# Running sums of the layer norms in PSUM tiles of half the tokens, and a third buffer for modulation columns

## The chip, the cores and the metric

The kernel runs on one core of one Trainium2 chip, as one launch. The metric is the device time of that launch in microseconds, as the median of several runs. The engines of the core are TensorE (PE), VectorE (DVE), ScalarE (ACT), GpSimd (POOL) and SyncE (SP), which here issues the transfers. Each has its own queue and works through it in order; a semaphore tells one engine that another has finished a step. SBUF is the working memory of 128 partitions, PSUM the memory that PE writes its products to. PSUM has eight banks, and one bank holds a tile of 128 x 512 fp32 numbers.

## The reference

Two post-norm layers over 512 tokens of 1024 channels, with fp32 data. Layer 0 mixes the tokens with two recurrent heads (SSD and HGRN2), layer 1 with a convolution module; each is followed by a gated MLP with a 3 x 3 convolution over the token grid. The vectors m (scales, shifts and gates per channel, "modulation") come from a conditioning vector. What matters here is cut from it:

```python
s_c = jax.nn.silu(c)
for l in range(DEPTH):
    m = (s_c @ ada_w[l] + ada_b[l]).reshape(-1, 6, 1, D_MODEL)
    h = modulate(x, m[:, 0], m[:, 1])
    ...  # y = mixer(h) for l = 0, convolution module for l = 1
    x = layer_norm(ALPHA * x + m[:, 2] * y, post_ln_g[l, 0], post_ln_b[l, 0])
    x = layer_norm(ALPHA * x + m[:, 5] * conv_glu_ffn(modulate(x, m[:, 3], m[:, 4]), ...),
                   post_ln_g[l, 1], post_ln_b[l, 1])
return x
```

So there are four layer norms over the channels, each behind a matrix product whose result is scaled by a modulation vector and added to x. A fifth norm lies inside the convolution module and isn't touched by the change.

## The kernel before

x lies transposed in SBUF: channels on the partitions, in KT = 8 blocks of 128 channels x T = 512 tokens (`self.x[:, i, :]`). The program runs through the stages mixer, MLP of layer 0, convolution module, MLP of layer 1. Every matrix product keeps fp32 accuracy by three matmuls of rounded numbers (`mm3w`, lines 214 to 216): high weight x high input, high weight x low input, low weight x high input.

**Weights.** They stream through in tiles of 128 x 512 (four blocks of 128 x 128, in the order in which PE uses them), numbered over the whole program. `_wload` issues the load on SP (line 182, tile `wraw`), casts the high part on ACT (line 184, `whi`) and subtracts on POOL (line 188, `wlo = wraw - whi`, two inputs in SBUF). There are six buffers of each kind, so a tile's load waits until the tile six before has been worked up, and a cast until PE has used the tile six before.

**Modulation.** One column of m is 512 KB of weights, 128 x 1024 numbers. Its load is issued on SP (line 270, tile `ada`, from the pool `adap`), and DVE multiplies it by the conditioning and sums it in one instruction (line 273). During the output product of the mixer (`wout`, 16 blocks of input) twelve columns are made (`ADA_OUT`). `adap` has two buffers there (line 799).

**A norm.** For each block i of 128 channels, `fm` or `group` makes the product in a PSUM bank (tiles `ps` or `psg`; `psh` for half the tokens) of the pool `mm`, which has five banks. In the output product all five are used at once, by the blocks 0 to 4 (NW1 = 5, tiles `psg`); block 5 is the first that needs one of them again. `residual` (line 909, DVE) makes x = ps * m + x. `ln_add` collects what the norm needs: ACT squares the block (line 929, tile `sq`; for block 0 straight into the sum, line 926), and DVE adds the block to a1 (line 930) and the square to a2 (line 931). a1 and a2 are SBUF tiles of 128 x 512, so both inputs of these adds lie in SBUF. The last blocks (2 in the output and down products, 4 in the second convolution product `cw2`) are made by halves of 256 tokens: first all of them for tokens 0 to 255, then for 256 to 511. In the second half, or during the next product, hooks (`stats_later`) place the first half's statistics between PE's matmuls.

**Statistics.** `ln_sums` sums a1 and a2 over the partitions with eight small matmuls by a column of ones (line 945, tile `sm` in PSUM); DVE makes the mean and 1/sqrt(variance) from them with 15 tiny instructions (lines 948 to 951 and 256 to 261, tiles `st` and `rs`). `ln_spread` lets PE turn `st` and `rs` into a tile `pb` in PSUM that holds them for all partitions (line 961). `pb` has two slots in the pool `lnps`, of one bank each, one for each half of the tokens. `normalise` in `post` then goes through the blocks: DVE x - pb and x * pb (lines 1031, 1032), ACT the scaled and shifted high part `h1hi` (line 1034) and the whole number `h` in PSUM (line 1038; line 1036 on DVE for some), DVE the low part `h1lo = h - h1hi` (line 1039). With the first of them the next product's `group` starts (tiles `psg`).

What stands in which order on each engine is decided by the tile framework's scheduler from its own costs and the pools' buffers, apart from the hooks.

Of the kernel before, what the change touches and what calls it, by code (L numbers as in the profile page):

```python
# [147 lines left out]
class Net:  # L148
# [645 lines left out]
    def merge(self, mx, ox, y, o, so, acth):  # L794
# [4 lines left out]
        self.adap = op.enter_context(self.pool("adap", 2))  # L799
# [59 lines left out]
        ln = self.ln_start()  # L859
        for i in range(NW1):  # L860
            self.ln_add(ln, i, self.residual(bk[i], 0, 2, i))
# [7 lines left out]
    def project(self, ln, w, act, kt, layer, j, tail, then=None, first=0):  # L869

        tail, keep = tail
        for i in range(first, KT - tail):
            ps = self.fm(self.mm, w, i * P, act, kt=kt)
            self.ln_add(ln, i, self.residual(ps, layer, j, i))
            if then:
                then(i)
        last = range(KT - tail, KT)
        kept = {}
        ln.append([])
        for t0, t1 in HALVES:  # L880
            for i in last:
                ps = self.mm.tile([P, t1 - t0], F32, tag="mm", name="psh")
                blocks = kept.get(i) or [self.wblock((w, k * P, i * P)) for k in range(kt)]
                if i >= KT - keep:
                    kept[i] = blocks
                for k in range(kt):
                    self.mm3w(ps, blocks[k], [a[:, t0:t1] for a in act(k)], k == 0, k == kt - 1)
                self.ln_add(ln, i, self.residual(ps, layer, j, i, t0, t1), t0, t1)
            if t1 < T:
                self.stats_later(ln, t0, t1, 9, 12)  # L890
            last = last[::-1]
        self.flush()
# [19 lines left out]
    def ln_start(self):  # L912
        a1 = self.work.tile([P, T], F32, tag="a1", name="a1", bufs=1)
        a2 = self.work.tile([P, T], F32, tag="a2", name="a2", bufs=1)
        return [a1, a2, {}]

# [19 lines left out]
    def ln_sums(self, ln, t0, t1):  # L936
# [5 lines left out]
        sm = self.lnps.tile([P, 3 * n], F32, tag="sm", name="sm")  # L942
        for j, a in enumerate((a1, a2)):
            for c in range(n):
                nc.tensor.matmul(sm[:, j * n + c:j * n + c + 1], a[:, t0 + c * P:t0 + (c + 1) * P], self.ones[:, 0:1], start=True, stop=True)
# [107 lines left out]
    def ffn(self, layer):  # L1053
# [31 lines left out]
        ln = self.ln_start()  # L1085
# [6 lines left out]
    def conformer(self):  # L1092
# [106 lines left out]
        ln = self.ln_start()  # L1199
        for i in range(NC1):  # L1200
            self.ln_add(ln, i, self.residual(bk[i], 1, 2, i))
# [58 lines left out]
```

## Time and profile before

| | |
|---|---|
| median of 3 runs | 1749.44 us (1749.41 to 1750.38) |
| profiled execution | 1749.62 us |
| its span, first to last instruction | 1747.9 us |
| mean granted clock of PE | 0.993 |
| PE busy | 1702.3 us |
| DVE busy | 1243.4 us |
| ACT busy | 849.8 us |
| POOL busy | 523.9 us |
| line 188 on POOL | 380 tiles, 1330 ns each |
| bytes moved | 192 MB on SP's queue |

In rows of the profile a first number is the start in us from the start of the span, then the duration, the engine, the line, the operation, "out<-in" by the program's names with shapes (partitions x elements), and in brackets the idle time before it and what ended that. Rows of a line's view give the number of instructions, their shortest, median and longest duration in ns, and where the first and the last start. Rows of a stretch of time give its length and the busy time of PE, PE's weight loads, DVE, ACT and POOL (number of instructions in brackets), then the granted clock of PE, the DMA's share and GB/s.

### The profile page before, as it was taken

Reading aid. Unit: us, or ns where it says so; the run is one execution under the profiler, and the core shown is the slowest. Engines: PE = TensorE matmul, PEld = TensorE weight load, DVE = VectorE, ACT = ScalarE, POOL = GpSimd, SP = SyncE. Lnnn points to the kernel's source line nnn. Section 1 sums busy time; section 2 is a strip of 40 time slices with the busy share of each in tenths; the row PEclk is TensorE's granted clock in tenths of the full one; section 3 lists DMA queues with packets and bytes.
Section 4 is the critical chain, followed back from the end, with each engine's and each line's share of the span. In section 5 each row is a group of like instructions: output and inputs, shape, how many; then the busy total and the mean of one; then the engine's idle time right before and its main releaser. Section 6 shows DMA issues by size and latency. Waiting matters only on the chain.

```text
span 1747.9 us, 26471 instructions
## 1 busy us (share of the span) xinstructions
PE 1702.3 (97%) x9574; PEld 1461.9 (84%) x9574; DVE 1243.4 (71%) x2380; ACT 849.8 (49%) x1714; POOL 523.9 (30%) x434
## 2 busy tenths in 40 slices
PE   7999999999999999999999999999999899999997
PEld 5987768989999998798888888988899788888886
DVE  7778987979696894678777741478888876666124
ACT  3556775444444453355434322399635643333223
POOL 4400000000000001545444444533425344444453
PEclk9999999999999999999999999999999999999998
DMA  9721102444444235634334343321213233333332
GB/s 363 241 70 49 31 19 90 145 142 149 132 147 132 96 103 155 213 88 130 110 109 123 110 134 96 109 73 55 61 31 89 87 93 97 98 98 98 97 97 79
DMA packets 92194, 194.02 MB, mean 111 GB/s; under 512 B 10496, under 2 KB 13568, under 8 KB 92064
## 3 DMA queue, kind: packets, MB, share of 16 engines
q1 hardware_dynamic: 92016, 192.21, 35.5%
q8 instruction: 75, 1.23, 0.3%
q14 instruction: 55, 0.45, 0.1%
q0 software_dynamic: 48, 0.13, 0.0%
HBM read 190.21 MB, written 2.10 MB: 110 GB/s over the span
## 4 chain that ended last, share of the span: by engine, by line
PE 88%; DVE 6%; DMA 1%; ACT 1%; issue 1%; POOL 0%; ACTq 0%; POOLq 0%; DVEq 0%
PE ps L214 18%; PE ps L216 18%; PE ps L215 18%; PE lev L744 3%; PE psz L234 2%; PE psz L235 2%; PE psz L233 2%; PE seg L645 2%; PE psh L214 2%; PE psh L216 2%; PE psh L215 2%; PE psg L215 1%; PE psv L234 1%; PE psv L235 1%; PE psv L233 1%; DMA ada<-adaw 1%
## 5 line engine op out<-in xcount | busy, mean ns | idle before, releaser
L188 POOL TENSOR_TENSOR wlo<-wraw,whi 128x512 fp32r<-128x512 f32 x380 | 503.7, 1330 | 1183.0 <-ACT whi L184 1158.9
L184 ACT CAST whi<-wraw 128x512 fp32r<-128x512 f32 x488 | 300.6, 619 | 494.6 <-PE ps L215 243.3
L214 PE MATMUL ps<-h1hi,whi 128*128 128x512 f32 x768 | 299.1, 389 | 0.8 <-DVE acc L1076 0.8
L216 PE MATMUL ps<-h1hi,wlo 128*128 128x512 f32 x768 | 299.1, 389 | 0.3 <-POOL wlo L188 0.3
L215 PE MATMUL ps<-h1lo,whi 128*128 128x512 f32 x768 | 298.9, 389 | 0.0
L1076 DVE SCALAR_TENSOR_TENSOR acc<-ps,pcol,acc 128x441 f32<-128x441 f32 (+2 forms) x320 | 222.3, 695 | 57.2 <-ACT acc L1068 47.7
L216 PEld LDWEIGHTS ps<-h1hi,wlo 128*128 128x128 f32 x768 | 144.2, 188 | 31.0 <-POOL wlo L188 1.2
L214 PEld LDWEIGHTS ps<-h1hi,whi 128*128 128x128 f32 x768 | 144.2, 188 | 30.8 <-issue 1.6
L215 PEld LDWEIGHTS ps<-h1lo,whi 128*128 128x128 f32 x768 | 144.2, 188 | 29.4
L273 DVE CUSTOM_DVE_ANT_0 junk<-ada,sc,pcol 128x1024 bf16<-128x1024 f32 x80 | 107.7, 1346 | 16.8 <-DMA ada<-adaw 16.8
L909 DVE SCALAR_TENSOR_TENSOR x<-ps,mod,x 128x512 f32<-128x512 f32 x14 | 10.5, 750 | 140.2 <-PE ps L216 140.2
L188 DVE TENSOR_TENSOR wlo<-wraw,whi 128x512 fp32r<-128x512 f32 x108 | 73.9, 691 | 42.5 <-ACT whi L184 42.1
L214 PE MATMUL ps<-ghi,whi 128*128 128x512 f32 x264 | 102.7, 389 | 0.0
L215 PE MATMUL ps<-glo,whi 128*128 128x512 f32 x264 | 102.7, 389 | 0.0
L216 PE MATMUL ps<-ghi,wlo 128*128 128x512 f32 x264 | 102.7, 389 | 0.0
L1168 DVE SCALAR_TENSOR_TENSOR cr<-u,pcol,cr 128x511 f32<-128x511 f32 (+20 forms) x156 | 98.0, 703 | 1.4 <-ACT cr L1151 1.2
L214 PE MATMUL ps<-hhi,whi 128*128 128x512 f32 x240 | 97.9, 408 | 0.0
L215 PE MATMUL ps<-hlo,whi 128*128 128x512 f32 x240 | 96.7, 403 | 0.0
L216 PE MATMUL ps<-hhi,wlo 128*128 128x512 f32 x240 | 96.2, 401 | 0.0
L987 DVE TENSOR_TENSOR glo<-acc,ghi 128x512 fp32r<-128x512 f32 x44 | 55.8, 1268 | 28.2 <-ACT ghi L986 28.0
L233 PE MATMUL psz<-whi,hhi 128*128 128x256 f32 (+1 forms) x224 | 67.6, 302 | 0.0
L234 PE MATMUL psz<-wlo,hhi 128*128 128x256 f32 (+1 forms) x224 | 67.3, 301 | 0.0
(358 smaller groups left out, 4153.1 us busy)
## 6 DMA issues: line engine op xcount, KB each, us to landing
wraw<-wst SPq DMA_DIRECT2D x488, 256.0 KB, 2.6
ada<-adaw SPq DMA_DIRECT2D x104, 512.0 KB, 3.6
xk<-xT SPq DMA_DIRECT2D x8, 256.0 KB, 7.7
x<-xT SPq DMA_DIRECT2D x8, 256.0 KB, 5.1
out<-n SPq DMA_DIRECT2D x16, 128.0 KB, 1.7
xk<-ctxT SPq DMA_DIRECT2D x8, 128.0 KB, 4.0
sc<-rows SPq DMA_DIRECT2D x1, 512.0 KB, 3.6
scc<-rows SPq DMA_DIRECT2D x1, 512.0 KB, 7.5
```

Of the source, the lines that this page charges most:

```text
L184: nc.scalar.copy(hi, raw)
L188: eng.tensor_tensor(out=lo, in0=raw, in1=hi.bitcast(F32), op=ALU.subtract)
L214: mm(ps, w[0], a[0], start=start, stop=False)
L215: mm(ps, w[0], a[1], start=False, stop=False)
L216: mm(ps, w[1], a[0], start=False, stop=stop)
L233: mm(ps, a[0], w[0], start=start, stop=False)
L234: mm(ps, a[0], w[1], start=False, stop=False)
L235: mm(ps, a[1], w[0], start=False, stop=stop)
L273: nc.vector.tensor_tensor_reduce(out=junk, in0=raw, in1=self.sc if cond is None else cond, scale=1.0, scalar=self.pc("adab", n), op0=ALU.m ...
L987: return nc.vector.tensor_tensor(out=lo, in0=x, in1=hi.bitcast(F32), op=ALU.subtract)
L1076: nc.vector.scalar_tensor_tensor(out=o, in0=grid(pg)[:, r0 + dy - 1:r1 + dy - 1, c0 + dx - 1:c1 + dx - 1], scalar=wcol(dy, dx), in1=o, op0 ...
L1168: nc.vector.scalar_tensor_tensor(out=acc[:, t0:t1], in0=u[:, t0 + d:t1 + d], scalar=self.pc("cdw", tap * 8 + i), in1=acc[:, t0:t1], op0=AL ...
```

## The change

The functions `lnp_start` and `lnp_add` are new and take the place of `ln_start` and `ln_add` in the four norms above. The sums are kept in two PSUM tiles `ap`, one for each half of the tokens, with the tag `pb`: they lie in the slots in which the broadcasts of the same norm come to lie later. Each tile holds the sum of x in its first 256 columns and that of the squares in the others. A block of 512 tokens is now added by four DVE instructions of 256 columns (lines 940 and 941, two each) where there were two of 512; block 0's square is written by two ACT instructions. The last block's add of each half writes its sums to SBUF (`a1`, `a2`), where the matmuls of `ln_sums` read them. Over the program 36 adds of 512 columns and 40 of 256 become 112 of 256. The second part is one number: `adap` has three buffers in the output product. Lines behind the new functions stand 29 further down.

```diff
--- before.py
+++ after.py
@@ -796,7 +796,7 @@
         TT = nc.vector.tensor_tensor
         op = self.stack()
         mp = op.enter_context(self.pool("mop"))
-        self.adap = op.enter_context(self.pool("adap", 2))
+        self.adap = op.enter_context(self.pool("adap", 3))
         ohi = mp.tile([P, 16, T], F32R, name="ohi")
         olo = mp.tile([P, 16, T], F32R, name="olo")
         ps_ = self.stack()
@@ -856,9 +856,9 @@
         for k in range(KT):
             nc.sync.dma_start(out=self.x[:, k, :], in_=self.A["xT"][k])
             nc.scalar.mul(self.x[:, k, :], self.x[:, k, :], ALPHA)
-        ln = self.ln_start()
+        ln = self.lnp_start()
         for i in range(NW1):
-            self.ln_add(ln, i, self.residual(bk[i], 0, 2, i))
+            self.lnp_add(ln, i, self.residual(bk[i], 0, 2, i))
         self.project(ln, "wout", lambda k: (ohi[:, k, :], olo[:, k, :]), 16, 0, 2, TAIL_W, first=NW1)
         op.close()
         mx.close()
@@ -871,7 +871,7 @@
         tail, keep = tail
         for i in range(first, KT - tail):
             ps = self.fm(self.mm, w, i * P, act, kt=kt)
-            self.ln_add(ln, i, self.residual(ps, layer, j, i))
+            self.lnp_add(ln, i, self.residual(ps, layer, j, i))
             if then:
                 then(i)
         last = range(KT - tail, KT)
@@ -885,7 +885,7 @@
                     kept[i] = blocks
                 for k in range(kt):
                     self.mm3w(ps, blocks[k], [a[:, t0:t1] for a in act(k)], k == 0, k == kt - 1)
-                self.ln_add(ln, i, self.residual(ps, layer, j, i, t0, t1), t0, t1)
+                self.lnp_add(ln, i, self.residual(ps, layer, j, i, t0, t1), t0, t1, last=i == last[-1])
             if t1 < T:
                 self.stats_later(ln, t0, t1, 9, 12)
             last = last[::-1]
@@ -910,9 +910,35 @@
         return self.x[:, i, :]
 
     def ln_start(self):
+
         a1 = self.work.tile([P, T], F32, tag="a1", name="a1", bufs=1)
         a2 = self.work.tile([P, T], F32, tag="a2", name="a2", bufs=1)
         return [a1, a2, {}]
+
+    def lnp_start(self):
+
+        a = [self.lnps.tile([P, 2, T // 2], F32, tag="pb", name="ap", bufs=2) for _ in HALVES]
+        o = [self.work.tile([P, T], F32, tag=tag, name=tag, bufs=1) for tag in ("a1", "a2")]
+        return [a, [t[:].rearrange("p (j t) -> p j t", j=2) for t in o], {}]
+
+    def lnp_add(self, ln, i, r, t0=0, t1=T, last=False):
+        nc = self.nc
+        a, o, rs = ln[:3]
+        if t0 == 0:
+            rs[i] = r
+        sq = None
+        if i:
+            sq = self.work.tile([P, t1 - t0], F32, tag="t", name="sq")
+            nc.scalar.activation(out=sq, in_=r[:, t0:t1], func=AF.Square)
+        for (h0, h1), ah, oh in zip(HALVES, a, o):
+            if not t0 <= h0 < t1:
+                continue
+            if not i:
+                nc.scalar.activation(out=ah[:, 1, :], in_=r[:, h0:h1], func=AF.Square)
+                continue
+            out = oh if last else ah
+            nc.vector.tensor_tensor(out=out[:, 0, :], in0=rs[0][:, h0:h1] if i == 1 else ah[:, 0, :], in1=r[:, h0:h1], op=ALU.add)
+            nc.vector.tensor_tensor(out=out[:, 1, :], in0=ah[:, 1, :], in1=sq[:, h0 - t0:h1 - t0], op=ALU.add)
 
     def ln_add(self, ln, i, r, t0=0, t1=T, eng=None):
         nc = self.nc
@@ -940,6 +966,9 @@
         n = (t1 - t0) // P
 
         sm = self.lnps.tile([P, 3 * n], F32, tag="sm", name="sm")
+        if isinstance(a2, list):
+            both, t0 = a2[t0 > 0], 0
+            a1, a2 = both[:, 0, :], both[:, 1, :]
         for j, a in enumerate((a1, a2)):
             for c in range(n):
                 nc.tensor.matmul(sm[:, j * n + c:j * n + c + 1], a[:, t0 + c * P:t0 + (c + 1) * P], self.ones[:, 0:1], start=True, stop=True)
@@ -1082,7 +1111,7 @@
                 self.next_x(i - 1)
             if layer == DEPTH - 1 or i % 3 == 0:
                 self.ada_some(1)
-        ln = self.ln_start()
+        ln = self.lnp_start()
         self.project(ln, f"dn{layer}", lambda k: (ghi[:, k, :], glo[:, k, :]), FT, layer, 5, TAIL_D, lambda i: self.ada_some(0 if layer or i > 3 else self.ADA_DOWN))
         fx.close()
         self.hx.close()
@@ -1196,9 +1225,9 @@
             add(*HALVES[1])
             self.stats_later(ln, *HALVES[1], 8, 9, lambda p: normed(*HALVES[1], p))
         bk = self.group("cw2", [i * P for i in range(NC1)])
-        ln = self.ln_start()
+        ln = self.lnp_start()
         for i in range(NC1):
-            self.ln_add(ln, i, self.residual(bk[i], 1, 2, i))
+            self.lnp_add(ln, i, self.residual(bk[i], 1, 2, i))
         self.project(ln, "cw2", self.act, KT, 1, 2, TAIL_C, first=NC1)
         cx.close()
         self.hx.close()
```

The order of PE's matmuls is the same but for some transposes, and POOL's is the same. What moves on SP and DVE is shown at two places.

SP's queue in the output product, from weight tile 143 on (`wraw143`; `ada82` to `ada87` and `ada72` to `ada75` are the third to the twelfth of the twelve modulation columns, `x` blocks of x that are loaded there). Before:

```order
L182 DMA wraw143_7447<-wst 128x512
L270 DMA ada82_7293<-adaw 128x1024
L270 DMA ada83_7297<-adaw 128x1024
L182 DMA wraw144_7465<-wst 128x512
L182 DMA wraw145_7483<-wst 128x512
L270 DMA ada84_7301<-adaw 128x1024
L270 DMA ada85_7305<-adaw 128x1024
L182 DMA wraw146_7501<-wst 128x512
L857 DMA x_7278<-xT 128x512
L270 DMA ada86_7309<-adaw 128x1024
L270 DMA ada87_7313<-adaw 128x1024
L182 DMA wraw147_7519<-wst 128x512
```

With the change:

```order
L182 DMA wraw143_7447<-wst 128x512
L270 DMA ada83_7297<-adaw 128x1024
L270 DMA ada84_7301<-adaw 128x1024
L270 DMA ada85_7305<-adaw 128x1024
L270 DMA ada86_7309<-adaw 128x1024
L270 DMA ada87_7313<-adaw 128x1024
L270 DMA ada72_7317<-adaw 128x1024
L270 DMA ada73_7321<-adaw 128x1024
L270 DMA ada74_7325<-adaw 128x1024
L270 DMA ada75_7329<-adaw 128x1024
L182 DMA wraw144_7465<-wst 128x512
L182 DMA wraw145_7483<-wst 128x512
```

The third column's load, `ada82`, has moved up, ahead of weight tile 128. The nine others now stand in one piece ahead of weight tile 144, the first that block 5 uses; before, they alternated with the tiles 144 to 148 and with blocks of x.

DVE's queue where the first half of the second convolution product's norm is applied and the second half's residuals come in (`rs` is 1/sqrt(variance) of the first half; `a_13559` and `a_13560` are a1 and a2, `a_13588` is both). Before:

```order
L261 SCALAR_TENSOR_TENSOR rs<-vt,sm 128x2
L1031 TENSOR_TENSOR x<-x,pb 128x256
L1032 TENSOR_TENSOR x<-x,pb 128x256
L1031 TENSOR_TENSOR x<-x,pb 128x256
L909 SCALAR_TENSOR_TENSOR x<-psh,mod,x 128x256
L1032 TENSOR_TENSOR x<-x,pb 128x256
L930 TENSOR_TENSOR a_13559<-a_13559,x 128x256
L931 TENSOR_TENSOR a_13560<-a_13560,sq 128x256
L1031 TENSOR_TENSOR x<-x,pb 128x256
L1032 TENSOR_TENSOR x<-x,pb 128x256
L1031 TENSOR_TENSOR x<-x,pb 128x256
```

With the change:

```order
L261 SCALAR_TENSOR_TENSOR rs<-vt,sm 128x2
L1060 TENSOR_TENSOR x<-x,pb 128x256
L1061 TENSOR_TENSOR x<-x,pb 128x256
L909 SCALAR_TENSOR_TENSOR x<-psh,mod,x 128x256
L1060 TENSOR_TENSOR x<-x,pb 128x256
L940 TENSOR_TENSOR ap<-ap,x 128x256
L1061 TENSOR_TENSOR x<-x,pb 128x256
L941 TENSOR_TENSOR ap<-ap,sq 128x256
L1060 TENSOR_TENSOR x<-x,pb 128x256
L1061 TENSOR_TENSOR x<-x,pb 128x256
L909 SCALAR_TENSOR_TENSOR x<-psh,mod,x 128x256
```

The residual of the second to last half block stands one row earlier, and its two adds stand between instructions of `normalise` where they stood behind each other; the instructions themselves are the same in number here.

## The prediction

> **What bounds the kernel now.** I read the page first, then the list of waits on TensorE (PE), then the time line at each wait.
>
> ```profile
> span 1747.9 us, 26471 instructions
> PE 1702.3 (97%) x9574; PEld 1461.9 (84%) x9574; DVE 1243.4 (71%) x2380; ACT 849.8 (49%) x1714; POOL 523.9 (30%) x434
> ```
>
> PE is busy for 97% of the span. The change takes no matmul away, so it can only give back PE's waits, and the time in which PE ran at a low clock. The waits list (releaser; us in total, times, longest):
>
> ```profile
> PE pb L961 <- DVE rs L261: 5.0, 4, 2.3
> PE sm L945 <- DVE a L930: 4.5, 3, 1.9
> PE ps L214 <- DVE x L909: 3.9, 1, 3.9
> PE psg L214 <- ACT h1hi L1034: 3.4, 3, 1.6
> ```
>
> These 16.8 us, with the half-clock time behind them, are all that can be won. The third row is one stall after the output product; the others are in the norms.
>
> **Part 1, the third modulation buffer.** The stall, with the work before it on DVE:
>
> ```profile
> 693.42 1.27 DVE L273 CUSTOM_DVE_ANT_0 junk<-ada,sc,pcol 128x1024 bf16<-128x1024 f32 x1
> ...
> 724.79 1.28 DVE L273 CUSTOM_DVE_ANT_0 junk<-ada,sc,pcol 128x1024 bf16<-128x1024 f32 x1 [1.43 <-DMA ada<-adaw]
> ...
> 726.00 2.06 DVE L909 SCALAR_TENSOR_TENSOR x<-psg,mod,x 128x512 f32<-128x512 f32 x3
> ```
>
> ```profile
> 726.89 0.47 PE L214 MATMUL ps<-ohi,whi 128*128 128x512 f32 x1 [3.94 <-DVE x L909]
> ```
>
> All five banks of the matmul pool hold products. The next one (block 5) waits until the residual of bank 0 has read it, and that stands on DVE behind twelve reductions, which wait for their loads: 14.2 us in all.
>
> ```profile
>   DMA ada<-adaw: 14.2, 9
> ...
> DMA to landing us min/median/max: 3.4/4.3/5.5
> ```
>
> ```profile
> wraw<-wst SPq DMA_DIRECT2D x11, 256.0 KB, 4.8
> ```
>
> (The last row is of the weight tiles in 690 to 727: count, size, us to landing.) With two buffers a load starts when the reduction two before has ended, so two loads take about 4.3 + 1.3 us, 2.8 each. With three it is (4.3 + 1.3)/3 = 1.9 us. The third load is now on its way before 691, the fourth starts at 693.4, when the first reduction has ended and the second starts, and lands at 697.7. Eight more at 1.9 us and 1.3 for the last end the chain at about 714. Is there bandwidth for it?
>
> ```profile
> 690.00:727.00 37.00, 33.06 (x147) 27.06 (x146) 22.60 (x33) 11.74 (x21) 19.14 (x11) 1.00 0.83 268
> 0.00:20.00 20.00, 7.86 (x22) 5.74 (x22) 9.14 (x14) 8.71 (x12) 9.74 (x12) 1.00 0.85 318
> ```
>
> Nine loads of 0.52 MB in 20 us are 236 GB/s, below the 268 of this window and the 318 of the start, and no weight tile is interleaved with them any more. Bank 0 is complete some 2.7 us before the other four, at 720.2, its residual takes 0.75, and PE arrives at 722.96: the cover is 2 us of PE, and six more before the chain is late. What is late next is weight tile 144, the first of block 5: it now stands on SP behind all twelve loads. Its issue comes when reduction 9 has ended, about 708; the tiles landed in 4.8 us here (median), and a cast and a subtraction follow, the one on POOL of 1.3 us as below, so it is ready at 715, 8 us ahead. Tiles 145 to 148 follow at a bandwidth that brings 0.26 MB in 1 us, against 2.7 us of PE for each; the x blocks behind them are needed only after 724. The stall of 3.9 us goes. Behind it PE ran at half clock:
>
> ```profile
> 727.60:731.00 3.40, 3.40 (x9) 2.68 (x9) 3.40 (x4) 1.65 (x4) 2.44 (x2) 0.51 0.39 122
> ...
> 1140.70:1144.10 3.40, 3.40 (x18) 3.40 (x17) 2.97 (x16) 2.86 (x9) 0.00 (x0) 0.50 0.24 78
> 1365.80:1369.20 3.40, 3.40 (x19) 3.34 (x18) 3.32 (x12) 3.34 (x8) 0.00 (x0) 0.52 0.01 2
> ```
>
> (The eighth number is the granted clock.) 3.4 us at half clock cost 1.7. With no stall before it, I count that as gained: **5.6 us**; bounds 0 (rival A) and 5.7.
>
> **Part 2, the sums in PSUM.** Why do the sums delay PE? DVE's adds of two SBUF tiles are stretched:
>
> ```profile
> L930 DVE TENSOR_TENSOR a<-a,x x34: 414/693/1766, 729.6 to 1733.5; 128x256 f32<-128x256 f32 x20, 128x512 f32<-128x512 f32 x14
> L931 DVE TENSOR_TENSOR a<-a,sq x42: 407/679/1789, 729.0 to 1734.1; 128x256 f32<-128x256 f32 x24, 128x512 f32<-128x512 f32 x18
> L1039 DVE TENSOR_TENSOR h1lo<-h,h1hi x48: 408/424/426, 763.4 to 1386.6; 128x256 fp32r<-128x256 f32 x48
> L909 DVE SCALAR_TENSOR_TENSOR x<-psh,mod,x x20: 471/483/486, 745.4 to 1733.0; 128x256 f32<-128x256 f32 x20
> L1138 DVE SCALAR_TENSOR_TENSOR u<-ps,pcol,sg x7: 739/750/759, 1165.0 to 1280.6; 128x512 f32<-128x512 f32 x7
> ```
>
> The same 256 columns take 0.41 us or up to 1.5. L1039 and L909, which have one operand in PSUM (h lies there), never vary. The time line shows who stretches them:
>
> ```profile
> 1135.59 2.52 POOL L188 TENSOR_TENSOR wlo<-wraw,whi 128x512 fp32r<-128x512 f32 x2 [0.21 <-ACT whi L184]
> ...
> 1136.02 0.42 DVE L1039 TENSOR_TENSOR h1lo<-h,h1hi 128x256 fp32r<-128x256 f32 x1
> ...
> 1137.41 0.98 DVE L930 TENSOR_TENSOR a<-a,x 128x256 f32<-128x256 f32 x1
> ```
>
> While POOL subtracts (1135.59 to 1138.11, two tiles), L1039 runs at full speed, and L930, both inputs in SBUF, ends only after it. The new adds each have one input in PSUM. The price of one that also writes PSUM over 256 columns is not in the trace. Below it is bounded by L1039's 0.42, above by L1138, which reads and writes PSUM over twice the columns, 0.75. L909 is nearest in size: I take 0.46.
>
> The full-width adds, 36 of 512 columns, become 72: 36 x (0.92 - 0.68) = 8.6 us more on DVE if none had been stretched. That lies under PE, for whose products DVE waits 140 us at L909:
>
> ```profile
> L909 DVE SCALAR_TENSOR_TENSOR x<-ps,mod,x 128x512 f32<-128x512 f32 x14 | 10.5, 750 | 140.2 <-PE ps L216 140.2
> ```
>
> Only the sums that PE waits for count.
>
> *Down product of layer 0* (the sums' tile in 1124 to 1140, and PE's wait):
>
> ```profile
> L930 DVE TENSOR_TENSOR a<-a,x x2: 983/1227/1471, 1127.7 to 1137.4; 128x256 f32<-128x256 f32 x2
> L931 DVE TENSOR_TENSOR a<-a,sq x2: 407/958/1509, 1129.1 to 1138.6; 128x256 f32<-128x256 f32 x2
> ```
>
> ```profile
> 1138.54 0.58 PE L945 MATMUL sm<-ones,a 128*128 128x1 f32 x4 [1.93 <-DVE a L930]
> ```
>
> Three adds of 1.47, 1.51 and 0.98 us, 3.96, become 1.38: 2.6 us come back, and the wait of 1.93 goes. The half-clock stretch at 1140.7 follows it, with no other wait inside; I count 1.2 of its 1.7. **3.1** (0 to 3.6).
>
> *Second convolution product.*
>
> ```profile
> 1352.98 1.45 DVE L930 TENSOR_TENSOR a<-a,x 128x256 f32<-128x256 f32 x1
> ...
> 1354.42 1.46 DVE L931 TENSOR_TENSOR a<-a,sq 128x256 f32<-128x256 f32 x1
> ...
> 1358.70 1.31 DVE L930 TENSOR_TENSOR a<-a,x 128x256 f32<-128x256 f32 x1
> 1359.94 1.50 DVE L931 TENSOR_TENSOR a<-a,sq 128x256 f32<-128x256 f32 x1
> ```
>
> ```profile
> 1356.39 0.43 PE L961 MATMUL pb<-tri,rs 128*128 128x128 f32 x2 [2.01 <-DVE rs L261]
> 1361.79 0.62 PE L214 MATMUL psg<-h1hi,whi 128*128 128x256 f32 x3 [1.14 <-ACT h1hi L1034]
> 1363.76 1.02 PE L945 MATMUL sm<-ones,a 128*128 128x1 f32 x8 [1.35 <-DVE a L930]
> ```
>
> The first pair stands inside the chain that makes rs: 2.0 us shorter, which is PE's 2.01. The second pair delays the last residual and its add: of the 1.35 about 1.15 go, since the square on ACT is still behind h1hi. The 1.14 stays: ACT makes h1hi after a cast that waits for PE itself. Half of the 1.7 us of half clock at 1365.8: 0.85. **4.0** (0 to 4.9).
>
> *Output product.*
>
> ```profile
> 758.82 1.40 DVE L931 TENSOR_TENSOR a<-a,sq 128x256 f32<-128x256 f32 x1
> ...
> 765.84 1.50 DVE L931 TENSOR_TENSOR a<-a,sq 128x256 f32<-128x256 f32 x1
> ```
>
> ```profile
> 760.35 0.43 PE L961 MATMUL pb<-tri,rs 128*128 128x128 f32 x2 [0.52 <-DVE rs L261]
> ```
>
> The two stretched adds hold up rs and sums; beside the 0.52 PE waits 0.29 and 0.16 in the same time line. **1.0**; the 1.6 us for h1hi at 777 follows the broadcast directly and stays.
>
> *Last product.* L909, L930 and L931 start last at 1733.0, 1733.5 and 1734.1, one behind the other, unstretched: **0**.
>
> The broadcasts need the sums' slots free; each half's last add has read its slot before its sums start, so no wait is added.
>
> By the Trainium skill (TensorE: Matmul & The Clock Gate, What's actually happening) the clock drops after an idle window of a free-running 3.4 us. The stretches above lie on such a grid and are as long, which agrees; but the waits of 1.93 and 1.35 us fill no whole window, so by the rule's words their stretches need not go with them, and the sum would be 2.05 smaller. No row decides it.
>
> Against the change speaks VectorE: DVE Perf Modes (the TRN2 errata section) of the Trainium skill: a fixed cost falls on each instruction, so tiles of 512 are better than two of 256. Two adds of 0.41 against one of 0.68 agree. On the path the sum would lose a further 36 x 0.14 = 5 us; the 140 us of waiting for PE say that it is off it.
>
> **Sum.** 5.6 + 3.1 + 4.0 + 1.0 = 13.7 us. The profiled execution took 1749.62 us (span 1747.9), the median is 1749.44, 0.2 below: **1735.7 us**.
>
> **Rivals.**
> A. *The stall stays*: the loads get no faster (two in flight already share 268 GB/s), or tile 144 comes as late as bank 0 did. For it: 0.83 of the DMA's time is busy. Against: 318 GB/s elsewhere. Then 8.1 us: 1741.3.
> B. *PSUM adds cost 0.75.* A pair takes 1.5 instead of 0.9, and half of the norms' gain goes; the last product loses 0.65. I make it 5.6 + 2.3 + 1.4 + 0.5 - 0.65 = 9.2: 1740.3.
> C. *The norms gain nothing*, because the chain over ACT (h1hi, h, each waiting for DVE and back) takes the wait's place. For it: three waits on h1hi, 3.4 us. Against: the sums wait for adds, not for ACT. Then 5.6: 1743.8.
> D. *Slower: an add that reads and writes one PSUM bank takes 1.0 us or more.* In the second convolution product 20 adds stand before the first sums; unstretched, DVE has some 5 us to spare there, so beyond 0.46 + 5/20 = 0.7 us each the sums come late, 6 us at 1.0; the output product has 24 and loses 2.4, the end and the second halves 3. With 5.6 gained at the stall it decides from about 0.9; at 1.0 about +6: 1755. Against: L1138 takes 0.75 for twice the columns.
>
> **Chances.** Forecast 0.60, A 0.13, B 0.14, C 0.08, D 0.05. The forecast's own range is 1732 to 1739; with A and B, 1732 to 1742.5. A change within 0.2%, 3.5 us, can't be told from none: faster than 1745.9 holds for all but D and the late part of C: 0.92; same 0.04; slower 0.04.
>
> **What would show it.** The new adds at 0.42 to 0.50 us with no stretched ones; no wait of PE on L909 near 723 and full clock after it; reductions ended by about 714; the sums' waits at 1138 and 1363 and the broadcast's at 1356 gone, that for h1hi still there; the end from the last matmul unchanged. Wrong: adds above 0.7, a wait of PE on a weight's cast or subtraction near 723, or half-clock stretches that stay.

## The result

The changed kernel takes **1734.76 us** (median, 1734.36 to 1736.75), the kernel before, measured beside it, 1749.43 us (1745.98 to 1750.38): a ratio of 0.9912, with an interval of 0.99 to 0.9925. The forecast was 1735.7 us. The profiled execution took 1734.44 us with a span of 1732.7, 15.2 less than before.

The page of the kernel after, its head:

```profile
span 1732.7 us, 26538 instructions
PE 1696.8 (98%) x9574; PEld 1458.9 (84%) x9574; DVE 1220.2 (70%) x2416; ACT 849.9 (49%) x1718; POOL 520.0 (30%) x434
```

DVE has 36 instructions more and is busy 23 us less. PE is busy for 5.5 us less with the same matmuls; two stretches at half clock fewer make 3.4 us of it. The list of PE's waits (releaser; us in total, times, longest):

```profile
PE psg L214 <- ACT h1hi L1063: 4.3, 3, 1.6
PE pb L990 <- DVE rs L261: 2.1, 1, 2.1
PE pc L214 <- DVE cr L1202: 2.0, 1, 2.0
PE sm L974 <- DVE a L940: 1.1, 1, 1.1
```

The wait on L909 is gone from the list. Of the four waits for rs and the three for the sums one each is left, both in the last norm. The waits for h1hi have grown from 3.4 to 4.3.

The new adds, by line (shortest, median, longest in ns):

```profile
L940 DVE TENSOR_TENSOR ap<-ap,x x40: 417/425/433, 727.7 to 1710.7; 128x256 f32<-128x256 f32 x40
L940 DVE TENSOR_TENSOR ap<-x x8: 418/886/1522, 724.9 to 1627.1; 128x256 f32<-128x256 f32 x8
L940 DVE TENSOR_TENSOR a<-ap,x x8: 415/424/425, 745.9 to 1718.4; 128x256 f32<-128x256 f32 x8
L941 DVE TENSOR_TENSOR ap<-ap,sq x48: 415/423/433, 727.0 to 1711.6; 128x256 f32<-128x256 f32 x48
```

With one input in PSUM no add takes over 0.433 us. Only the second row's eight, block 1's x added to block 0's, still have both inputs in SBUF, and they are still stretched, to 1.52.

The output product, by stretches of time (PE, its weight loads, DVE, ACT, POOL; clock, DMA share, GB/s), and DVE's time line there:

```profile
690.00:727.00 37.00, 37.00 (x165) 30.61 (x164) 26.75 (x36) 14.33 (x27) 18.98 (x13) 1.00 0.81 270
727.00:733.00 6.00, 6.00 (x28) 4.98 (x27) 6.00 (x17) 2.54 (x5) 3.85 (x4) 1.00 0.81 268
```

```profile
699.62 2.13 DVE L273 CUSTOM_DVE_ANT_0 junk<-ada,sc,pcol 128x1024 bf16<-128x1024 f32 x1
701.84 2.32 DVE L273 CUSTOM_DVE_ANT_0 junk<-ada,sc,pcol 128x1024 bf16<-128x1024 f32 x1
...
716.18 1.28 DVE L273 CUSTOM_DVE_ANT_0 junk<-ada,sc,pcol 128x1024 bf16<-128x1024 f32 x1 [2.34 <-DMA ada<-adaw]
...
720.39 2.10 DVE L909 SCALAR_TENSOR_TENSOR x<-psg,mod,x 128x512 f32<-128x512 f32 x3 [2.92 <-PE psg L216]
```

PE is busy for all of the 37 us and at full clock behind them. The order has turned round: the residual of bank 0 now waits 2.92 us for PE's product.

PE's rows in the down product of layer 0 and in the second convolution product, where waits stood before:

```profile
1129.00 0.51 PE L974 MATMUL sm<-ones,a 128*128 128x1 f32 x4
```

```profile
1343.47 0.38 PE L990 MATMUL pb<-tri,rs 128*128 128x128 f32 x2
...
1348.58 0.62 PE L214 MATMUL psg<-h1hi,whi 128*128 128x256 f32 x3 [1.14 <-ACT h1hi L1063]
1349.04 0.95 PE L974 MATMUL sm<-ones,a 128*128 128x1 f32 x8
...
1358.40 0.38 PE L990 MATMUL pb<-tri,rs 128*128 128x128 f32 x2
1360.38 0.62 PE L214 MATMUL psg<-h1hi,whi 128*128 128x256 f32 x3 [1.60 <-ACT h1hi L1063]
```

The waits of 1.93, 2.01 and 1.35 us have gone, the 1.14 stays, and the last wait is 1.60 where it was 0.65 before:

```profile
1375.80 0.61 PE L214 MATMUL psg<-h1hi,whi 128*128 128x256 f32 x3 [0.65 <-ACT h1hi L1034]
```

Where the 15.2 us came from is read off by taking the same matmul in both traces (a stage's first `sm` or `ps`), and how much earlier it starts:

| matmul | before | after | earlier by | gained in between | predicted |
|---|---|---|---|---|---|
| first sums of the output norm | 754.25 | 748.46 | 5.79 | 5.8 | 5.6 |
| first `ps` behind that norm | 799.62 | 792.05 | 7.57 | 1.8 | 1.0 |
| first sums of down product 0 | 1120.74 | 1113.17 | 7.57 | 0 | 0 |
| first sums in the convolution module | 1310.85 | 1299.87 | 10.98 | 3.4 | 3.1 |
| first sums behind `cw2` | 1348.67 | 1337.69 | 10.98 | 0 | 0 |
| first sums of down product 1 | 1718.85 | 1703.75 | 15.10 | 4.1 | 4.0 |
| end of the span | 1747.9 | 1732.7 | 15.2 | 0.1 | 0 |

### The profile page after: what moved, and what is told of

Same layout as the page of the kernel before. It is cut to its first block, busy times and chain, and to the rows that moved or that the text cites. A ratio compares the mean times of both kernels' runs of the same rounds, so it can differ in the third digit from the quotient of the medians.

```text
span 1732.7 us, 26538 instructions
## 1 busy us (share of the span) xinstructions
PE 1696.8 (98%) x9574; PEld 1458.9 (84%) x9574; DVE 1220.2 (70%) x2416; ACT 849.9 (49%) x1718; POOL 520.0 (30%) x434
## 4 chain that ended last, share of the span: by engine, by line
PE 93%; DVE 3%; ACT 1%; issue 0%; POOL 0%; ACTq 0%; POOLq 0%; DVEq 0%
PE ps L214 18%; PE ps L216 18%; PE ps L215 18%; PE lev L744 3%; PE psg L215 2%; PE psg L216 2%; PE psg L214 2%; PE psh L214 2%; PE psh L215 2%; PE psh L216 2%; PE psz L235 2%; PE psz L234 2%; PE psz L233 2%; PE seg L645 2%; PE psv L234 1%; PE psv L235 1%
## 5 line engine op out<-in xcount | busy, mean ns | idle before, releaser
L909 DVE SCALAR_TENSOR_TENSOR x<-ps,mod,x 128x512 f32<-128x512 f32 x14 | 10.5, 750 | 139.0 <-PE ps L216 139.0
L1016 DVE TENSOR_TENSOR glo<-acc,ghi 128x512 fp32r<-128x512 f32 x44 | 56.0, 1273 | 28.2 <-ACT ghi L1015 28.0
```

The lines of the kernel that those rows point to most:

```text
L1016: return nc.vector.tensor_tensor(out=lo, in0=x, in1=hi.bitcast(F32), op=ALU.subtract)
```

## The experiments

Two things differ from execution to execution of one kernel and are taken out below. One is PE's first matmul, which starts between 10.8 and 12.9 us, as soon as ACT has made its input; so beside the medians the table gives the span *from the first matmul* of the profiled execution. The other is the number of half-clock stretches from 700 us to the last norm, each 3.4 us long; what decides them comes last. (Between the start-up and 700 us only "last pair in PSUM" had one, at 21.5 us.) Each row's profile is of one execution, and its median of 4 to 11. The mixer, in which nothing was changed, still scatters: from PE's first matmul to the first of the output product it took 655.2, 656.3 and 655.5 us in the three executions of the change, so a microsecond in this column is no gain by itself.

| run | median us (range) | ratio to before (interval) | from the first matmul | half-clock stretches |
|---|---|---|---|---|
| before, beside each of them | 1749.4 to 1751.1 | 1 | 1736.7 | 4 |
| the change | 1734.76 (1734.36-1736.75) | 0.9912 (0.99-0.9925) | 1721.5 | 2 |
| changed again | 1735.7 (1734.91-1736.37) | 0.9915 (0.9901-0.993) | 1723.6 | 2 |
| changed, third time | 1736.95 (1735.83-1737.68) | 0.9918 (0.9903-0.9932) | 1722.5 | 1 |
| third buffer alone | 1744.86 (1743.58-1747.03) | 0.9974 (0.9963-0.9985) | 1732.1 | 3 |
| PSUM sums alone | 1741.57 (1740.74-1743.37) | 0.9956 (0.9943-0.9968) | 1728.5 | 3 |
| halves in SBUF | 1746.77 (1744.87-1747.94) | 0.9982 (0.9973-0.9991) | 1733.0 | 5 |
| POOL writes only | 1727.74 (1727.53-1728.44) | 0.9875 (0.986-0.989) | 1715.7 | 1 |
| four buffers | 1736.42 (1734.76-1737.02) | 0.9921 (0.9904-0.9937) | 1723.4 | 2 |
| last pair in PSUM | 1734.25 (1734.13-1734.7) | 0.9908 (0.9892-0.9925) | 1721.6 | 1 |
| casts after first half | 1736.28 (1735.19-1738.3) | 0.992 (0.9905-0.9935) | 1722.4 | 2 |
| both of these | 1734.16 (1731.85-1735.08) | 0.9905 (0.989-0.992) | 1720.7 | 1 |
| filled waits | 1734.45 (1733.19-1736.56) | 0.9908 (0.9891-0.9925) | 1720.4 | 0 |
| filled, and last pair | 1733.42 (1733.16-1734.13) | 0.9899 (0.9884-0.9914) | 1719.2 | 0 |

### Each part by itself

The third buffer alone is the kernel before with one number changed:

```diff
-        self.adap = op.enter_context(self.pool("adap", 2))
+        self.adap = op.enter_context(self.pool("adap", 3))
```

> The kernel before with one number changed: three modulation buffers in the output product. Theory: the two parts act in different places and add up. The stall behind the reductions and its half-clock stretch go, the first sums of the output product's norm start about 5.8 us earlier, all waits in the norms stay: 1743.7 us (1742.5 to 1745). Rival (the buffer matters only together with the cheaper adds, since both are work of DVE): less than 3 us, above 1746.5.

The PSUM sums alone are the changed kernel with that number back at 2.

> The changed kernel with two modulation buffers in the output product again. Theory: the stall of about 3.9 us on the residual is back with half clock behind it, and the norms keep their gain of 9 us: 1740.3 us (1739 to 1742), and the two parts' gains sum to the whole. Rival (parts not additive): both single gains sum to less than 12 or more than 17 us.

The third buffer alone gained 4.6 us from the first matmul. PE's waits in it:

```profile
PE pb L961 <- DVE rs L261: 5.0, 4, 2.3
PE sm L945 <- DVE a L930: 4.5, 3, 1.9
PE psg L214 <- ACT h1hi L1034: 3.4, 3, 1.6
```

The three are those of before to the tenth, and the stall on L909 is gone. At the first sums (749.59 against 754.25, with a start of 12.29 against 11.20) this gives 4.7 + 1.1 = 5.8 us, as in the whole change. Behind the down product 1.2 of it are lost again, since there the half clock lasted for two stretches and not one:

```profile
1130.50:1133.90 3.40, 1.47 (x14) 1.30 (x12) 3.40 (x9) 3.40 (x9) 3.30 (x19) 1.00 0.57 183
1133.90:1137.30 3.40, 3.40 (x18) 3.40 (x18) 1.33 (x7) 1.71 (x4) 1.31 (x1) 0.50 0.65 166
1137.30:1140.70 3.40, 3.40 (x18) 3.40 (x17) 2.62 (x15) 3.38 (x11) 0.00 (x0) 0.50 0.03 10
```

With the PSUM sums alone the stall is back, and the norms' gain is there (8.2 us from the first matmul):

```profile
726.56 0.47 PE L214 MATMUL ps<-ohi,whi 128*128 128x512 f32 x1 [3.87 <-DVE x L909]
```

So the parts add up: 4.6 + 8.2 = 12.8 us, against 13.1 to 15.2 for the three profiled executions of the whole; by the medians 5.1 + 8.4 = 13.6 us, against 14.2 to 14.9. The rest is within what the stretches differ by: of the two parts' executions each has one that the kernel before has not, here behind the down product, there at 1287 us.

### Is it PSUM, or the smaller adds?

The rival to "one input in PSUM" is that adds of 256 columns interleave better. Here the split is kept and the sums stay in SBUF:

```diff
-        a = [self.lnps.tile([P, 2, T // 2], F32, tag="pb", name="ap", bufs=2) for _ in HALVES]
         o = [self.work.tile([P, T], F32, tag=tag, name=tag, bufs=1) for tag in ("a1", "a2")]
-        return [a, [t[:].rearrange("p (j t) -> p j t", j=2) for t in o], {}]
+        o = [t[:].rearrange("p (j t) -> p j t", j=2) for t in o]
+        return [o, o, {}]
```

> The changed kernel (three buffers, adds of 256 columns, same order of writing) with the sums kept in the SBUF tiles a1 and a2 instead of PSUM. Theory (DVE's adds of two SBUF tiles are held up by POOL's subtraction): adds are stretched to 1.0 to 1.5 us again, PE waits for them as before, and the split costs nothing by itself: 1743 to 1745.5 us. Rival (the gain in the norms came from the split into halves and from the new order of DVE): adds at 0.42 us or stretched ones that nobody waits for, 1734 to 1737 us.

Measured 1746.77, a little above the first range; the rival falls. Its adds and PE's waits:

```profile
L940 DVE TENSOR_TENSOR a<-a,x x48: 411/426/1526, 731.2 to 1731.5; 128x256 f32<-128x256 f32 x48
```

```profile
PE sm L974 <- DVE a L940: 4.5, 3, 1.9
PE pb L990 <- DVE rs L261: 4.2, 4, 2.3
```

Same instructions, same shapes, and the longest is 1.53 us where it is 0.43 with the sums in PSUM; the waits for the sums are those of before, those for rs 4.2 in place of 5.0 us. The split by itself shows no gain: from the first matmul the run is 0.9 us longer than the third buffer alone, with two half-clock stretches more, and its median is 1.9 us higher.

### Is it POOL that stretches them?

That was inferred from overlaps. Here POOL doesn't read SBUF for the weights from the output product on: it writes zeros in place of the subtraction. (Nine adds of 512 columns in the convolution module's own norm still stand on POOL, between 1184 and 1255 us.) The sums are those of the kernel before (512 columns, SBUF), with the third buffer. The low parts of those weights are left out of the products.

```diff
-        eng = nc.gpsimd if self.lo_pool else nc.vector
-        eng.tensor_tensor(out=lo, in0=raw, in1=hi.bitcast(F32), op=ALU.subtract)
+        if self.lo_pool:
+            nc.gpsimd.memset(lo.bitcast(F32), 0.0)
+        else:
+            nc.vector.tensor_tensor(out=lo, in0=raw, in1=hi.bitcast(F32), op=ALU.subtract)
```

> The kernel before with three modulation buffers, its sums in SBUF and adds of 512 columns, but POOL fills wlo with zeros instead of subtracting (it reads nothing; the low parts of the weights are left out of the products from the output product on). Theory (POOL's reads of SBUF hold up DVE's adds of two SBUF tiles): no add is stretched, 0.42 us for 256 and 0.68 for 512 columns, and the norms' waits go as with PSUM: 1733 to 1737 us. Rival (any work of POOL in SBUF, or PSUM's own speed): adds above 0.9 us remain while POOL writes, and the time stays at 1741 to 1745 us.

The adds by line, and one that ran beside POOL:

```profile
L932 DVE TENSOR_TENSOR a<-a,x x34: 415/426/693, 721.8 to 1712.3; 128x256 f32<-128x256 f32 x20, 128x512 f32<-128x512 f32 x14
```

```profile
733.62 0.69 DVE L933 TENSOR_TENSOR a<-a,sq 128x512 f32<-128x512 f32 x1
733.63 0.52 POOL L188 MEMSET wlo<- 128x512 f32 x1 [0.91 <-PE psh L218]
```

The longest add of x over 512 columns takes 0.69 us (1.77 before), and the longest of the squares 0.70 (1.79). POOL's instruction is shorter too (0.53 against 1.30), but it isn't the shorter overlap alone: this one covers three quarters of the add and adds nothing to it. PE's waits for the norms are down to those of the last norm, nearly as with PSUM:

```profile
PE pb L963 <- DVE rs L263: 2.2, 2, 2.0
PE sm L947 <- DVE a L932: 1.1, 1, 1.1
```

The unstretched adds agree with the Trainium skill (SBUF — State Buffer, Who interferes with whom): a DVE instruction with two SBUF inputs gets into the way of a GpSimd instruction that reads SBUF, not of one that only writes it.

The time, 1727.74, was lower than expected by 5 us and more, so the expectation was wrong about what else hangs on this. PE's list in this run has no wait for `cr` any more (2.0 us), and other instructions with two SBUF inputs are no longer stretched: the low parts in the MLPs (`glo`, 44 of 512 columns) took 692 ns on average in place of 1273, the filter's products in the convolution module 667 in place of 702. How the rest divides stays open; this kernel leaves out part of the products.

### Would a fourth buffer give more?

```diff
-        self.adap = op.enter_context(self.pool("adap", 3))
+        self.adap = op.enter_context(self.pool("adap", 4))
```

> The changed kernel with four modulation buffers in the output product. Theory (three buffers already end the chain before the product does, so the stall is gone and more gives nothing): the reductions end a little before 717 us, PE waits for none of it, 1734 to 1736.5 us. Rival (the loads are bound by bandwidth: with four in flight each takes longer and the chain ends no earlier, or weight tile 144 comes late): the same end of the chain with longer loads, or a wait of PE near 723 us.

1736.42, no gain. The last reduction and the residual:

```profile
713.34 1.28 DVE L273 CUSTOM_DVE_ANT_0 junk<-ada,sc,pcol 128x1024 bf16<-128x1024 f32 x1 [0.48 <-DMA ada<-adaw]
...
720.63 2.10 DVE L909 SCALAR_TENSOR_TENSOR x<-psg,mod,x 128x512 f32<-128x512 f32 x3 [5.99 <-PE psg L216]
```

The chain ends 2.8 us earlier than with three, and all of it goes into DVE's wait for PE (5.99 against 2.92).

### What is left: the filter's last pair and the casts

Two waits that the change leaves were tried next, beside the changed kernel again.

> The changed kernel once more, as the measure for the three others on the same chip: 1734 to 1736 us. Theory of the scatter (a half-clock stretch of 3.4 us costs up to 1.7 us, and on which waits it falls depends on how a free-running grid lies): single runs spread over some 3 us, and the number of half-clock stretches in the profile need not be the two of the first profile. Rival (the stretches belong to the waits): again two, behind the same waits.

PE waits 2.0 us in the convolution module for the sum `cr`, at the end of a chain of filter products whose inputs `u` and `cr` lie in SBUF. For the last pair of blocks `u` now stays in the PSUM bank of its product:

```diff
-                    u = ct.tile([P, T], F32, tag="u", name="u")
+                    u = pa
```

> The changed kernel, and in the convolution module's last pair of blocks the gated input u stays in the PSUM bank of its product, where it had a tile in SBUF. Theory (DVE instructions with two SBUF inputs are held up by POOL wherever they stand): the 15 tap products at 1258 us that took 11.1 us (0.74 each) take 0.4 to 0.45 each, PE's wait of 2.0 us for them goes, 1731.5 to 1733.5 us. Rival (the held banks of PSUM stop PE's next products, or the wait goes over to another chain): 1734.5 us or more.

The filter's first products of the last pair on DVE, after, and in this run those up to 1268.8 us:

```profile
L1197 DVE SCALAR_TENSOR_TENSOR cr<-u,pcol,cr x15: 460/474/1511, 1258.6 to 1269.3; 128x256 f32<-128x256 f32 x8, 128x250 f32<-128x250 f32 x1, 128x249 f32<-128x249 f32 x1, 128x248 f32<-128x248 f32 x1
```

```profile
L1197 DVE SCALAR_TENSOR_TENSOR cr<-ps,pcol,cr x9: 475/484/485, 1263.0 to 1267.9; 128x256 f32<-128x256 f32 x9
```

The fifteen took 11.1 us, 0.74 on average, because five of them, those beside POOL's adds and subtractions, took 1.5 us each; the ten others took 0.46 to 0.47. With `u` in PSUM none takes over 0.485, though POOL was subtracting beside seven of these nine. The wait of 2.0 us is gone from PE's list; the one for the next product's first high part (line 1015) grew from 0.6 to 0.9. The median, 1734.25, is above the range of the theory. It is 1.45 us lower than that of the changed kernel beside it, the span from the first matmul 2.0 lower, and 3.2 from the output product's first matmul on (1064.1 against 1067.4 us), which leaves out the start; the intervals overlap.

The wait of 1.14 us for h1hi stands behind a weight cast on ACT. The next casts are asked for after the first half is normalised:

```diff
-        self.prefetch()
...
         normalise(*HALVES[0], ln[3][0])
+        self.prefetch()
```

> The changed kernel with the weight tiles ahead asked for after the first half's normalisation has been written down, not before it, so that ACT makes the first high parts ahead of casts. Theory (in the second convolution product the wait of 1.14 us for the high part comes from a cast queued before it that waits for PE): it goes, 1733 to 1734.5 us. Rival (casts come late and PE waits for weights, or for the next high part): 1735 us or more.

1736.28: a miss. ACT's rows and PE's:

```profile
1348.14 0.62 ACT L184 CAST whi<-wraw 128x512 fp32r<-128x512 f32 x1 [0.82 <-PE psh L215]
1348.67 0.60 ACT L1062 ACTIVATE h1hi<-x,cb,cg 128x256 fp32r<-128x256 f32 x1
```

```profile
1349.31 0.62 PE L214 MATMUL psg<-h1hi,whi 128*128 128x256 f32 x3 [1.14 <-ACT h1hi L1062]
```

The same cast stands ahead, and ACT's order around it is that of the changed kernel: the line that was moved isn't the one that asks for this tile. Both edits together:

> Both edits of the two others together. Theory: their gains add, 1730.5 to 1732.5 us. Rival (one chain behind both): no better than the better of the two alone.

1734.16, no better than the first of them alone: a miss as well, for the same reason.

### What decides the half clock

The stretches are all 3.4 us long. Within one execution their starts lie on one grid of 3.413 us; where the grid lies differs from execution to execution. Stretches of time after, and then of the changed kernel again (PE, weight loads, DVE, ACT, POOL; clock, DMA share, GB/s):

```profile
771.20:774.60 3.40, 3.40 (x18) 3.40 (x18) 3.04 (x10) 3.38 (x7) 0.45 (x1) 0.52 0.01 2
1281.90:1285.30 3.40, 3.40 (x32) 3.40 (x31) 1.52 (x4) 0.42 (x1) 0.00 (x0) 1.00 0.01 2
1358.30:1361.70 3.40, 1.50 (x11) 1.06 (x10) 2.81 (x8) 1.97 (x4) 0.00 (x0) 1.00 0.00 0
1361.70:1365.10 3.40, 3.40 (x19) 3.40 (x19) 3.03 (x9) 3.40 (x7) 0.31 (x1) 0.53 0.00 0
```

```profile
771.20:774.60 3.40, 2.88 (x20) 2.47 (x20) 3.03 (x10) 3.40 (x7) 0.00 (x0) 1.00 0.01 2
1281.90:1285.30 3.40, 3.40 (x17) 3.40 (x18) 1.86 (x5) 0.66 (x2) 0.00 (x0) 0.52 0.01 2
```

One program, and at 771 only the first execution has a half-clock stretch, at 1282 only the second. Counted over all grid windows between 700 us and the last norm, in the 14 executions of the table: all 20 windows in which PE was busy for 0.49 of the time or less (down to 0.19) were followed by a half-clock window. The 12 of 0.53 to 0.62 never were; of those above, five (0.63 to 0.69), and each of these five held eight of the sums' one-column matmuls, whose records may be longer than their work. In the last norm, which is left out of this count, seven windows of 0.52 to 0.67 were followed by half clock too, and each of them held eight such matmuls. So for windows with eight of them the rule isn't shown. The row 1358.30:1361.70 above, 1.50 of 3.40 us busy, shows a window of the first kind. So a wait of 1.6 us, with the shorter one for h1lo behind it, was enough where one grid window took it in whole, and did nothing where the grid divided it. In two executions the half clock lasted for two windows, though PE was busy all through the first of them, as in the rows of the third buffer alone; these two windows also held such one-column matmuls, and why the half clock went on stays open.

The test is to make PE busy in the two waits of 1.6 us for h1hi before the up products: ten matmuls by 256 columns of zeros, whose result the next matmul overwrites. ACT copies one column of rs into the zeros, so that they wait for rs and stand behind the second broadcast.

```diff
+        if mark:
+            self.nc.scalar.copy(self.fill[:, 0:1], r[:, 0:1])
...
+                if w.startswith("up"):
+                    for _ in range(FILL):
+                        self.nc.tensor.matmul(pss[0][:, t0:t1], blocks[KT - 1][0][0], self.fill, start=True, stop=True)
```

> The changed kernel once more, as the measure for the two others on the same chip: 1734 to 1736.5 us, with one to three half-clock stretches at places that need not be the former ones.

> The changed kernel, and in the two waits of 1.6 us for the first high part of the second half, ahead of the up products, ten matmuls of 256 columns by a tile of zeros, whose result the product's first matmul overwrites (they wait for the second half's rs, so they stand behind the broadcast). Theory (a stretch of the free-running grid of 3.4 us in which PE was busy for less than about half is followed by one at half clock): the stretches in question hold 2.6 instead of 1.5 us of work, no half clock follows them, each one avoided saves up to 1.7 us, 1732.5 to 1734.5 us. Rival (the half clock comes from the wait itself, or the added work delays the product): half-clock stretches behind these waits as before, 1735 us or more.

> The same together with the last pair's gated input in PSUM, which took away the wait of 2.0 us in the convolution module. Theory: both gains add, 1731 to 1733.5 us, and no half-clock stretch before the last norm in most executions. Rival: no better than 1734 us.

PE's rows at the first of the two waits, with the filling:

```profile
767.60 1.43 PE L1016 MATMUL psg<-fill,whi 128*128 128x256 f32 x10
769.45 0.62 PE L215 MATMUL psg<-h1hi,whi 128*128 128x256 f32 x3 [0.42 <-ACT h1hi L1073]
```

What is left of the wait of 1.60 us is 0.42; the rest is filled, and h1hi comes no earlier for it. No half-clock stretch is left before the last norm in either execution. At this wait a grid window (767.3 to 770.8) took in the whole of it: PE was busy for 0.79 of that window, and full clock followed, where 0.45 had been followed by half clock in the first execution of the change. That the run with the filling alone has no stretch at 1282 is not the filling's doing: there the grid divided the wait of 2.0 us for `cr`. The changed kernel took 1736.95 beside these runs, 0.45 above its range, with one stretch. 1734.45 is 2.5 us below the changed kernel beside it, 2.1 of it from the first matmul, but its range (1733.19 to 1736.56) and its interval overlap with that one's, so by the time alone the gain of the filling is not shown. With the last pair's `u` in PSUM it is 1733.42, 3.5 below, 3.3 from the first matmul. Its interval of 0.9884 to 0.9914 still overlaps that of the changed kernel beside it (0.9903 to 0.9932), but the ranges of the times don't touch (1733.16 to 1734.13, 1735.83 to 1737.68). By its median it is the fastest here that computes the whole reference.

## Why the prediction was right, and where not

**The whole: 13.7 us predicted, 14.2 to 14.9 measured** by the medians of the three runs of the change. No term came out smaller than forecast. That the total lies within a microsecond or so is in part luck: from the output product's first matmul on, the three profiled executions of this one program are 15.2, 14.1 and 14.4 us shorter than the one before, and their half-clock stretches lie at different waits.

**The stall of the output product: 5.6 predicted, 5.8 measured.** Right, and for its reason: three loads in flight brought the residual ahead of PE. The 5.8 lies a tenth above the bound of 5.7. Rival A, that the stall stays, has no wait to show. One step was off: the reductions ended at 717.4, not 714. From 693.4 on, where the prediction's count begins, three of them took 2.1 to 2.3 us in place of 1.3, those beside a subtraction on POOL; the last load was issued at 710.1 in place of about 708, and it took 5.9 us to land in place of 4.3. The reductions too read two tiles, and part 2's own reason was not applied to them. They explain at most the 2 us by which that load was issued late: with four buffers four were stretched from there on, and the chain still ended at 714.6. Weight tile 144 came late by as much: its subtraction ended at 719.2 and not at 715, 3.6 us ahead of PE and not 8. The residual still came in time, with 2.9 us to spare where six were counted.

**The add's price: 0.46 taken, 0.425 measured.** The lower bound, L1039's 0.42, was the right row: writing PSUM cost nothing that shows. Rivals B (0.75 us) and D (0.9 and more) fall with it. The prediction overlooked that block 1's sum of x still has two SBUF inputs; at up to 1.52 us no wait of PE stands behind it.

**Down product 0: 3.1 predicted, 3.4 measured.** The wait of 1.93 went. With it went nearly the whole 1.7 us at half clock, of which 1.2 was counted: in the window ahead of the stretch, 1137.3 to 1140.7, PE had been busy for 2.16 of 3.40 us, and now it is busy without a break there (1126.0 to 1133.0).

**Second convolution product: 4.0 predicted, 4.1 measured**, but not quite by its steps. The broadcast's wait gave 1.9 (2.0 predicted), and at the sums 1.5 more were gained (1.15) beside 0.3 ahead of them. The last term failed in its mechanism: of the half clock 0.85 was counted. It went whole between the sums and the second broadcast, but the order of PE changed there:

```profile
1363.76:1373.82 10.06, 10.06 (x71) 10.00 (x72) 7.99 (x32) 7.07 (x14) 0.00 (x0) 0.83 0.07 25
```

```profile
1349.04:1358.40 9.36, 9.36 (x81) 9.36 (x80) 8.45 (x33) 7.11 (x14) 0.34 (x1) 1.00 0.20 57
```

Between the same two matmuls, before and after: 71 matmuls at a mean clock of 0.83, 10.06 us; 79 at full clock, 9.36 us (the row's 81 include two that had begun before). The eight that now stand ahead of the broadcast used to stand behind it and filled most of the wait for h1hi. So PE's order did change by more than transposes, against what was said of it at the change: in the trace the small matmuls of the statistics stand at other places among the product's. From the broadcast to the first product it is 1.98 us in both (1373.82 to 1375.80, 1358.40 to 1360.38), the length of the chain over two normalising steps on DVE and h1hi on ACT; only what PE does in it has changed (eight matmuls start 0.12 us apart, 1.0 us). So 1.7 came back and 1.0 was given away as wait, and the new idle window at 1358.3 brought a stretch of half clock of its own, which cost 0.3 net by the up product. Rival C named this chain as the next bound. It was, for a small part: the sums' waits went first.

**Output product's norm: 1.0 predicted, 1.8 measured.** The waits of 0.52, 0.29 and 0.16 went. But at the three places 0.7, 0.7 and 0.3 us came back: the term was mis-sized because it took the listed waits alone, and the small matmuls beside a wait had been slower too (0.43 to 0.61 us where they now take 0.38 to 0.51).

**Last product: 0 predicted, 0.1 measured.** Its waits for the sums and for rs are those left in PE's list.

**The clock.** The Trainium skill's rule (TensorE: Matmul & The Clock Gate, What's actually happening), a free-running window of 3.4 us, holds: the stretches lie on such a grid. By its "idle window" the stretches behind the waits of 1.93 and 1.35 us need not have gone, and the sum would be 2.05 smaller; they went. No window before a stretch was idle here: PE was busy for 0.19 to 0.49 of most, and before these two, with one-column matmuls in them, for 0.63 and 0.64 by the records. The measurement decides. It also follows that a half-clock term of 0 to 1.7 us for each wait can't be forecast closer than by its chance: three executions of the changed kernel had two, two and one.

**The fixed cost of an instruction.** The Trainium skill's rule (VectorE: DVE Perf Modes, the TRN2 errata section) is seen: two adds of 0.425 against one of 0.68. As counted, the extra 0.17 us per pair lies where DVE waits for PE, and no term of the ledger shows a loss.

## What to carry to other kernels

When two engines share the work around a matmul pipeline, look for instructions of one shape whose durations spread (0.41 to 1.5 us): a longest far above the median points to a contention, and moving one operand to PSUM can remove it without changing the count of instructions. In a kernel that is PE-bound at 97%, price each remaining wait with its half-clock stretch, and after removing one look at what the scheduler has moved out of the next. Short waits that can't be removed may be worth filling with matmuls of zeros; here that took the stretches away, and a gain in time is not yet clear of the scatter.

## What the runs showed of the hardware

- A half-clock stretch needs no idle window: with 0.19 to 0.49 of a 3.413 us grid window busy it followed in 20 of 20 windows before the last norm, with 0.53 to 0.62 in none of 12. Windows with the eight one-column matmuls of the sums are an exception: there it followed at 0.52 to 0.69. Where the grid lies changes with each execution, so one program had a stretch at 771 in one and at 1282 in another.
- The modulation reduction (128 x 1024) is stretched like the adds: 1.28 us alone, up to 2.32 beside POOL's subtraction; and the subtraction in turn took up to 2.22 there, against 1.29.
- POOL writing 128 x 512 numbers without reading took 0.53 us and left a DVE add of 0.69 us beside it as it was.
- A filter product of 244 to 256 columns with both tensors in SBUF took 0.46 to 0.47 us, and 1.5 beside POOL's adds and subtractions; with one tensor in PSUM it took up to 0.485, beside the subtraction as well.
